# Which PSUM banks the last output-projection group takes in a hybrid decoder step

## The chip, the cores and the metric

The kernel runs on one core of one Trainium2 chip. The metric is device time in microseconds (us) of one execution. The engines are named as in the profile: PE is TensorE's matmul, PEld its weight load, DVE VectorE, ACT ScalarE, POOL GpSimd, SP SyncE, whose queue issues most loads. Time is told in us from the start of the span.

## What is computed

One layer of a decoder trunk for 512 prompt tokens and 8 single tokens of other sequences (520 columns in all, handled as two halves of 260): a SwiGLU feed-forward, a mixer with an output projection, a second SwiGLU, and a last norm. All is float32. Cut to what matters here:

```python
h = h + 0.5 * _swiglu(_rms_norm(h, ffn1_norm), ffn1_w_gate, ffn1_w_up, ffn1_w_down)
m, p, c, s = _hybrid_mixer(_rms_norm(h, mix_norm), ...)   # m = cat @ w_out, cat: pooled (512) and gated state-space (1024)
h = h + m                                                  # 1024 wide: 8 tiles of 128
h = h + 0.5 * _swiglu(_rms_norm(h, ffn2_norm), ffn2_w_gate, ffn2_w_up, ffn2_w_down)   # 2816 wide: 22 tiles f
```

## The kernel before

Features lie on the 128 partitions and tokens along the free axis, so `h` is 8 tiles (d = 0 to 7) of 128 x 520. A product in full precision is made of three matmuls of split operands: weights and inputs are each cut into a high part (a cast to the matmul's reduced format) and a low part (the rest), and high x high, high x low and low x high are added in a PSUM bank. The casts are made by ACT (`shi`, `whi`, `thi`), the low parts by DVE subtractions (`slo`, `wlo`, `tlo`) or, for some, by an accumulating DMA that POOL issues.

**The output projection** (`wout`) runs over three groups j of 512 input features and, in a group, over four weight loads d2, each for the two output tiles d = 2 d2 and 2 d2 + 1. For each d and each half b, twelve matmuls (eight at line 160, four at line 165) fill one bank, a tile named `wo{j}_{d}{b}`, and DVE adds it to `h` (line 1311). Below, `wo_50` is output tile 5, half 0, of the last group j = 2.

**The second feed-forward** (`Ffn` with i = 2) begins under that last group. Its first weight tile f = 0 is computed plainly in float32 (line 311, tiles `P_00` for the gate and `P_01` for the up projection; each float32 matmul shows as two rows in the trace), over four pairs j of input tiles (d = j and j + 4); `fin` squares and scales a finished `h` tile on ACT (`sq_f`, `xg_f`; the names of the pairs 0 to 3 end in 7345, 7379, 7505 and 7539), and `fill(j)` issues the pair's `P` matmuls and prepares its sums and differences (`xd_f`) with their high and low parts (`xth_f`, `xtl_f`) for the tiles f from 1 on. The order in which the stages are written is the string

```python
LAST_PLAN = "h0 h2 h1 n0 h3 n1 n2 n3"
```

where `h` is a call of `wout` with its d2 and `n` one of `fill`. So output tiles come in the order 0, 1, 4, 5, 2, 3, 6, 7.

The tiles f from 1 on save a multiplication by a seven-product scheme: a tile has an accumulator `A` (one bank) and a pair `BE` (two banks). Between products the partial sum in `A` is copied out by ACT (line 504), then the next product is added into the same bank. The last product of a tile f uses a quarter of its weights, `qs`, and is issued after the first product of tile f + 1. The first products of f = 1 use weights `whi_1a`, `shi_1c` and `shi_1d`; its third copy out of `A_1` goes to `ac_1_1`.

**Banks.** The pool that `open_f2` opens has eight banks: tag `ps` has two, tag `A` two, and tag `BE` two tiles of two banks. A tag's banks are taken in turn, and the next tile of a tag waits until the one two before it has been read. `P_00` and `P_01` take the two `BE` tiles. The tag `A` serves the accumulators of f = 1, 2 and so on.

**Order.** The program is written in the order of the plan, but the framework reorders instructions: a scheduler with a model of each engine decides the order on each engine's queue, apart from instructions that are pinned or made to be issued behind a given other. The queues themselves run in order. A change of buffers thus changes the order.

Of the kernel before, what the change touches and what calls it, by code (L numbers as in the profile page):

```python
# [897 lines left out]
def mixer(tc, ins, outs, e):  # L898
# [393 lines left out]
    def wout(cat, j, d2, fin=None):  # L1292
        src, name = ins["w_out"][j, d2], f"wo{j}{d2}"
        if (j, d2) in OUT_LOW_BY_DMA:
            raw = raw_tile(name)
            nc.sync.dma_start(out=raw, in_=src)
            wh, wl = e["weight_homes"](1024, name, wp, 3, ("whi", "wlo"))
            e["part_by_dma"](wh, wl, raw, src)
        else:
            wh, wl = load_unit(src, 1024, name, (*behind.get((j, d2), ()), *rows[-5:-4]) if (j, d2) == (2, 2)  # L1300
                               else behind.get((j, d2), ()))
        for d in (2 * d2, 2 * d2 + 1):
            for b, hs in enumerate(HALVES):
                if d != 1 or j != 2:
                    ps = bank(f"wo{j}_{d}{b}")
                else:
                    ps = e["ps"][0].tile([P, 512], F32, tag="A", bufs=2, name=f"wo{j}_{d}{b}")
                i = range((d % 2) * 4, (d % 2) * 4 + 4)
                mm_low_last(ps[:, :HB], *([ws(w, k) for k in i] for w in (wh, wl)),
                            *([cat[:, q, k, hs] for k in range(4)] for q in range(2)), True)  # L1310
                rows.append(nc.vector.tensor_tensor(out=h[:, d, hs], in0=ps[:, :HB], in1=h[:, d, hs], op=ALU.add).ins)  # L1311
                if fin is not None:
                    fin(d, b, hs)
# [49 lines left out]
    def outs_a():  # L1363
# [19 lines left out]
        "B": lambda j: ssd_b(*ssd(j)),  # L1383
        "z": zproj,
        "o": lambda j: wout(catp, 0, j),
        "G": gate,
        "H": gate_out,
        "g": lambda j: wout(cats[0], 1, j),
        "h": lambda j: wout(cats[1], 2, j, fin),
        "n": fill,  # L1390
        "e": lambda j: outs_a(),
# [101 lines left out]
```

## Time and profile before

| | us |
|---|---|
| median of 3 runs | 950.68 (949.75 to 951.92) |
| the profiled execution, its whole time | 952.73 |
| its span, from the first to the last instruction | 950.9 |
| mean granted TensorE clock | 0.997 |

The profile is of one execution. Busy time is the time in which an engine had an instruction under way; matmuls overlap, so the start of one row to the start of the next tells the cost of a matmul better than its length does. In the rows in order of time the columns are the start, the length, the engine, the line, the operation, the tile written and the tiles read, the shape and the number of instructions, and in brackets the idle time of the engine just before and what ended it.

### The profile page before, as it was taken

What the parts mean: (1) busy time and instruction counts of PE and PEld (TensorE: products, weight loads), DVE (VectorE), ACT (ScalarE), POOL (GpSimd) and SP (SyncE); (2) the same over time, 40 slices, a digit from 0 to 9 for tenths busy, and PEclk for the clock granted to TensorE, in tenths of its full rate; (3) what the DMA queues carried; (4) which work ended last, traced back from release to release, by engine and by line L of the source; (5) the groups of instructions that cost most, each with busy time, mean ns of one, the idle gap of its engine ahead of it and who ended that gap; (6) DMA issues with size and microseconds to landing.
All of it is one profiled execution on the core that took longest, in us unless ns stands there. A gap on an engine that the chain in (4) does not pass through costs nothing. (4 is left out here: it accounts for less than half of the span.)

```text
span 950.9 us, 19685 instructions
## 1 busy us (share of the span) xinstructions
PE 941.6 (99%) x7674; PEld 923.9 (97%) x7674; DVE 851.8 (90%) x1462; ACT 635.7 (67%) x1178; POOL 152.6 (16%) x230
## 2 busy tenths in 40 slices
PE   9999999999999999999999999999999999999996
PEld 8999999999999999999999899999999999999996
DVE  6899899998988698779998998999999999999986
ACT  7777756667566465475768745777776677766764
POOL 0011100100100002146251100111112101122120
PEclk9999999999999999999999999999999999999998
DMA  7666554455553335354364443546666655767642
GB/s 212 180 164 146 148 147 140 113 135 164 134 153 97 87 96 162 91 169 150 97 179 133 140 113 117 139 120 156 164 178 175 164 147 137 172 203 181 171 158 91
DMA packets 54123, 138.36 MB, mean 146 GB/s; under 512 B 7878, under 2 KB 16006, under 8 KB 54030
## 3 DMA queue, kind: packets, MB, share of 16 engines
q1 hardware_dynamic: 40046, 104.20, 34.6%
q0 software_dynamic: 13712, 32.78, 18.6%
q8 instruction: 60, 0.98, 0.4%
q14 instruction: 33, 0.27, 0.1%
q10 hardware_dynamic: 272, 0.13, 0.0%
HBM read 129.74 MB, written 7.34 MB: 144 GB/s over the span
## 5 line engine op out<-in xcount | busy, mean ns | idle before, releaser
L504 ACT COPY ac<-A 128x260 f32<-128x260 f32 x85 | 31.7, 373 | 34.6 <-PE A L165 16.4
L433 DVE TENSOR_TENSOR s<-raw 128x1024 f32<-128x1024 f32 x39 | 47.6, 1221 | 4.0 <-DMA raw<-in_w2gu 2.5
L504 ACT COPY ac<-BE 128x260 f32<-128x260 f32 x41 | 15.5, 377 | 33.4 <-PE BE L165 17.6
L151 PE MATMUL inx<-xh_mx,whi_inx 128*128 128x260 f32 x112 | 31.8, 284 | 0.0
L154 PE MATMUL inx<-xl_mx,whi_inx 128*128 128x260 f32 x112 | 31.6, 282 | 0.0
L155 PE MATMUL inx<-xh_mx,wlo_inx 128*128 128x260 f32 x112 | 31.6, 282 | 0.0
L1033 DVE SCALAR_TENSOR_TENSOR A<-U,h,A 128x544 f32<-128x544 f32 x36 | 28.4, 789 | 1.8 <-ACT A L1031 1.4
L311 PE MATMUL P<-x,raw 128*128 128x260 f32 x128 | 29.3, 390 | 0.0
L311 PEld LDWEIGHTS P<-x,raw 128*128 128x128 f32 x128 | 24.9, 196 | 3.9
L160 PE MATMUL wo<-catg,whi_wo 128*128 128x260 f32 x192 | 27.4, 285 | 0.0
L160 PEld LDWEIGHTS wo<-catg,whi_wo 128*128 128x128 f32 x192 | 24.8, 188 | 0.2
L139 ACT CAST thi<-raw 128x1024 fp32r<-128x1024 f32 (+1 forms) x14 | 14.2, 1014 | 15.5 <-PE wo L160 4.8
L1311 DVE TENSOR_TENSOR h<-wo,h 128x260 f32<-128x260 f32 x48 | 19.2, 423 | 4.9 <-PE wo L165 4.7
L1199 ACT ACTIVATE so<-br,sxdt 128x128 f32<-128x128 f32 x64 | 22.7, 375 | 1.2 <-DVE room L1201 0.7
L252 DVE TENSOR_TENSOR gs<-gq,gs 128x780 fp32r<-128x780 f32 (+1 forms) x28 | 23.2, 829 | 0.0
L151 PE MATMUL inz<-xh_mx,whi_inz 128*128 128x260 f32 x80 | 22.9, 287 | 0.0
L154 PE MATMUL inz<-xl_mx,whi_inz 128*128 128x260 f32 x80 | 22.7, 283 | 0.0
L155 PE MATMUL inz<-xh_mx,wlo_inz 128*128 128x260 f32 x80 | 22.6, 283 | 0.0
L512 DVE TENSOR_TENSOR BE<-BE,ac 128x260 f32<-128x260 f32 (+1 forms) x41 | 18.5, 451 | 3.1 <-PE BE L155 1.7
L151 PEld LDWEIGHTS inx<-xh_mx,whi_inx 128*128 128x128 f32 x112 | 21.1, 188 | 0.2 <-issue 0.2
L160 PE MATMUL A<-xth_f,qs 128*128 128x260 f32 x84 | 21.2, 283 | 0.0
L160 PE MATMUL A<-xtl_f,qs 128*128 128x260 f32 x84 | 21.2, 284 | 0.0
(3135 smaller groups left out, 4380.9 us busy)
## 6 DMA issues: line engine op xcount, KB each, us to landing
raw<-in_w2gu SPq DMA_DIRECT2D x44, 512.0 KB, 4.3
raw<-in_w1gu SPq DMA_DIRECT2D x41, 512.0 KB, 4.2
raw<-in_w_in SPq DMA_DIRECT2D x24, 512.0 KB, 3.6
raw<-in_w1d SPq DMA_DIRECT2D x16, 512.0 KB, 4.6
raw<-in_w2d SPq DMA_DIRECT2D x16, 512.0 KB, 4.3
raw<-in_w_out SPq DMA_DIRECT2D x12, 512.0 KB, 3.5
ab<-scr_acs SPq DMA_DIRECT2D x8, 512.0 KB, 6.3
h<-in_state_ssm SPq DMA_DIRECT2D x16, 256.0 KB, 3.7
```

What stands on the lines that cost most here:

```text
L151: first = nc.tensor.matmul(ps, whi, xhi, start=start, stop=False, **kw)
L154: nc.tensor.matmul(ps, whi, xlo, start=False, stop=False, **kw)
L155: nc.tensor.matmul(ps, wlo, xhi, start=False, stop=stop, **kw)
L160: mm = nc.tensor.matmul(ps, w, x, start=start, stop=False, **kw)
L252: low = nc.vector.tensor_tensor(out=lo, in0=s, in1=hi.bitcast(F32), op=ALU.subtract)
L311: mm = nc.tensor.matmul(self.banks[f, u][b][:, :HB], ws(self.raw[f][:, u], j + 4 * q), xg[:, slot[q]], start=j == q == 0, stop=j == 3 and ...
L433: nc.vector.tensor_tensor(out=s1, in0=diag, in1=up0, op=ALU.add)
L504: self.copied = nc.scalar.copy(keep, out[:, :HB]).ins
L512: nc.vector.tensor_tensor(out=be[:, s], in0=be[:, s], in1=a[:, s], op=ALU.add)
L1033: nc.vector.scalar_tensor_tensor(out=A[:, :n], in0=U[:, j : j + n], scalar=w(j), in1=A[:, :n], op0=ALU.mult, op1=ALU.add)
L1199: nc.scalar.activation(out=o[:, q], in_=br, func=AF.Copy, scale=sxdt[:, j, b : b + 1]))
L1311: rows.append(nc.vector.tensor_tensor(out=h[:, d, hs], in0=ps[:, :HB], in1=h[:, d, hs], op=ALU.add).ins)
```

## The change

In the last group, the two halves of every odd output tile (1, 3, 5, 7) take the two banks of tag `A`; the even ones keep the two banks of tag `ps`. Before, only output tile 1 took the banks of tag `A`, and the seven others shared those of tag `ps`.

```diff
         for d in (2 * d2, 2 * d2 + 1):
             for b, hs in enumerate(HALVES):
-                if d != 1 or j != 2:
+                if d % 2 == 0 or j != 2:
                     ps = bank(f"wo{j}_{d}{b}")
                 else:
                     ps = e["ps"][0].tile([P, 512], F32, tag="A", bufs=2, name=f"wo{j}_{d}{b}")
```

No instruction is added or removed. What the scheduler makes of it shows on PE first. Before, from the end of output tile 4 on, the fill of pairs 0 and 1 stands between the tiles (`thi`, `tlo` are weights, `catg` the projection's input, `xg_f` a pair's scaled input, a row with x2 is two matmuls):

```order
L165 MATMUL wo_41_7328<-catg_7093,tlo 128x260 x4
L311 MATMUL P_00_7451<-xg_f_7345,raw 128x260 x2
L311 MATMUL P_01_7456<-xg_f_7345,raw 128x260 x2
L160 MATMUL wo_50_7348<-catg_7093,thi 128x260 x8
L165 MATMUL wo_50_7348<-catg_7093,tlo 128x260 x4
L160 MATMUL wo_51_7362<-catg_7093,thi 128x260 x8
L165 MATMUL wo_51_7362<-catg_7093,tlo 128x260 x4
L311 MATMUL P_00_7451<-xg_f_7345,raw 128x260 x2
L311 MATMUL P_01_7456<-xg_f_7345,raw 128x260 x2
L311 MATMUL P_00_7451<-xg_f_7379,raw 128x260 x2
L311 MATMUL P_01_7456<-xg_f_7379,raw 128x260 x2
```

Now, at the end of the group on PE, the last tiles follow each other, and the fill of pairs 1, 2 and 3 comes behind them:

```order
L160 MATMUL wo_70_7508<-catg_7093,whi_wo_7470 128x260 x8
L165 MATMUL wo_70_7508<-catg_7093,wlo_wo_7471 128x260 x4
L160 MATMUL wo_71_7522<-catg_7093,whi_wo_7470 128x260 x8
L165 MATMUL wo_71_7522<-catg_7093,wlo_wo_7471 128x260 x4
L311 MATMUL P_00_7451<-xg_f_7379,raw 128x260 x4
L311 MATMUL P_01_7456<-xg_f_7379,raw 128x260 x4
L311 MATMUL P_00_7451<-xg_f_7505,raw 128x260 x2
```

Between these two places output tiles 5, 2 and 3 now run without a `P` matmul, and pair 0's eight `P` matmuls stand together behind tile 3. Of the 64 `P` rows of the trace, 40 stood ahead of the last tile, and 16 do now. Four matmuls of `A_1` that stood ahead of tile 7 now stand behind all of `P`.

On ACT the order moves too, also past the group's end. Before, at the first products of tile f = 1, the third copy out of `A_1` stands ahead of two casts of weights (`shi_2d` of tile 2 and `whi_3a` of tile 3; `gq_0` is the gate of f = 0):

```order
L504 COPY ac_1_0_7635<-A_1_7633 128x260
L139 CAST shi_2c<-s_2_2_7727 128x1024
L369 ACT_TABLE_LOAD
L369 ACTIVATE gq_0_7582<-gq_0_7582 128x2x260
L504 COPY ac_1_1_7636<-A_1_7633 128x260
L139 CAST shi_2d<-room 128x1024
L139 CAST whi_3a<-raw 128x1024
```

Now, at the same place on ACT:

```order
L504 COPY ac_1_0_7635<-A_1_7633 128x260
L139 CAST shi_2c<-s_2_2_7727 128x1024
L369 ACT_TABLE_LOAD
L369 ACTIVATE gq_0_7582<-gq_0_7582 128x2x260
L139 CAST shi_2d<-room 128x1024
L139 CAST whi_3a<-raw 128x1024
L504 COPY ac_1_1_7636<-A_1_7633 128x260
```

The copy now stands behind both casts. On DVE the evictions of line 1311 move ahead of the preparation of the pairs, and in the first tiles of the feed-forward some rows change places; on POOL one transfer (`wlo_1a`) moves ahead of another; the order on SP is the same.

## The prediction

> **What bounds the kernel now.** I read the page first, then the list of what TensorE waited for, then the table by stages around the change, then the rows in order of time.
>
> ```profile
> span 950.9 us, 19685 instructions
> PE 941.6 (99%) x7674; PEld 923.9 (97%) x7674; DVE 851.8 (90%) x1462; ACT 635.7 (67%) x1178; POOL 152.6 (16%) x230
> ```
> TensorE is busy for 99% of the span, so only two things can move the time: TensorE work, or a place where TensorE stands still. The list of its waits over the whole span (total, times, longest):
>
> ```profile
> PE warm L709 <- DVE eps L95: 1.1, 1, 1.1
> PE factor L870 <- PE psl L864: 0.6, 1, 0.6
> PE inz L151 <- DVE E L1278: 0.4, 1, 0.4
> PE psl L864 <- ACT sq_last L834: 0.3, 1, 0.3
> PE yo L1262 <- DVE hst L1275: 0.2, 1, 0.2
> PE px L1223 <- ACT X L1035: 0.2, 1, 0.2
> ```
> None is an output projection tile waiting for a bank. The stage, with the first five columns as busy time of PE, PEld, DVE, ACT and POOL (instructions), then the granted clock, DMA share and GB/s:
>
> ```profile
> 584.00:615.00 31.00, 31.00 (x205) 29.00 (x205) 27.17 (x46) 21.84 (x30) 4.99 (x6) 1.00 0.51 119
> 615.00:620.00 5.00, 5.00 (x43) 4.93 (x42) 4.97 (x5) 2.47 (x7) 0.00 (x0) 1.00 0.50 164
> 620.00:625.00 5.00, 5.00 (x44) 5.00 (x43) 5.00 (x8) 4.62 (x6) 0.00 (x0) 1.00 0.27 75
> ```
> TensorE is busy 31.00 of 31.00 us in the stretch in which the last group's tiles and the fill run. VectorE is nearly as full. Who waits for whom there is told by the group of the evictions (busy, mean ns | idle before, and what ended it):
>
> ```profile
> L1311 DVE TENSOR_TENSOR h<-wo,h 128x260 f32<-128x260 f32 x12 | 5.1, 424 | 2.2 <-PE wo L165 2.0
> ```
> VectorE waits 2.0 us for TensorE's tiles; TensorE waits for no eviction. With two banks the fill (`P`) stood between the tiles and covered the evictions.
>
> **The change part by part.** *Work on TensorE.* The same matmuls are issued, in other places: 40 of the 64 `P` rows and four of `A_1` stood ahead of the last tile, now only 16 do. Does it pay to break up a block less often?
>
> ```profile
> 584.66 1.92 PE L311 MATMUL P<-xg_f,raw 128*128 128x260 f32 x8
> 586.22 1.31 PE L160 MATMUL wo<-catg,thi 128*128 128x260 f32 x8
> 587.37 0.64 PE L165 MATMUL wo<-catg,tlo 128*128 128x260 f32 x4
> 587.84 1.13 PE L160 MATMUL wo<-catg,thi 128*128 128x260 f32 x8
> 589.28 3.67 PE L311 MATMUL P<-xg_f,raw 128*128 128x260 f32 x16
> 592.60 1.31 PE L160 MATMUL wo<-catg,whi_wo 128*128 128x260 f32 x8
> 594.23 1.12 PE L160 MATMUL wo<-catg,whi_wo 128*128 128x260 f32 x8
> ```
> From start to start, a tile alone takes 589.28 - 587.84 = 1.44. Eight `P` and a tile take 587.84 - 584.66 = 3.18, so the eight cost 1.74; sixteen and a tile take 594.23 - 589.28 = 4.95, so the sixteen cost 3.51. Twice 1.74 is 3.48: a switch costs nothing (-0.03). The longer first rows after `P` (1.31 for 1.12) are only an earlier start. Term: 0, bounds -0.1 and +0.1.
>
> *The banks.* `wo_50` now takes the bank of `wo_10`, and so on: each tile takes a bank whose eviction lies four tiles back, 5.7 us of TensorE time. An eviction is 0.42 (row above), and the longest queue that I find ahead of one on VectorE is some 2.5 us of other work; no wait. Term 0.
>
> *Fill and `A_1` behind the tiles.* Six tiles from 584.66 end at 593.3, 16 `P` at 596.8, four tiles at 602.6, then `P` for pairs 1 and 2 at 609.6. The last pair's scaled tiles need two evictions, a square and two scales behind `wo_71`, some 3 us of ACT and DVE work from 602.6, and are wanted at 609.6. The last `P` and the four rows of the sums of squares (0.22 each, as `P`) end at 614.0, `A_1`'s first product at 615.4; its bank is that of `wo_70`, long free. One new wait: VectorE's differences of pair 2 take the buffer of pair 1's scaled tile, whose `P` matmuls now run to 606.1 (before, they stood ahead of the last four tiles). Behind that wait VectorE has eleven operations, those of these two rows among them:
>
> ```profile
> 607.54 0.69 DVE L238 TENSOR_TENSOR xd_f<-xg_f 128x520 f32<-128x520 f32 x1
> 614.92 1.24 DVE L252 TENSOR_TENSOR xtl_f<-xd_f,xth_f 128x1040 fp32r<-128x1040 f32 x1
> ```
> Before, the stretch from the first to the end of the second was 8.6 us with one eviction and one addition more, about 1.0; so eleven from 606.2 end near 613.9, and with a wait for a cast that ACT can make only after its copy of `P_00`, at 615.2. The first matmul that needs it stands at 616.2. Before, it was late:
>
> ```profile
> 615.72 0.64 PE L165 MATMUL A<-xth_f,wlo_1a 128*128 128x260 f32 x4
> 616.21 0.39 PE L160 MATMUL BE<-xtl_f,shi_1c 128*128 128x260 f32 x1
> 616.44 0.64 PE L165 MATMUL BE<-xth_f,slo_1c 128*128 128x260 f32 x4
> ```
> 616.44 - 616.21 = 0.23 where two matmuls otherwise stand 0.12 apart: a gap of 0.11 as the operand ends at 616.16. It goes: -0.11, bounds -0.11 and +0.5 (VectorE 1.4 us later than I count).
>
> *What the order on ScalarE makes of it.* This is the largest term. `A_1`'s third copy (L504) must have read the bank before TensorE adds the last quarter (`qs`) into it. Before:
>
> ```profile
> 619.53 1.06 ACT L139 CAST shi_2c<-s 128x1024 fp32r<-128x1024 f32 x1 [0.58 <-PE BE L160]
> 620.60 1.28 ACT L369 ACT_TABLE_LOAD   x1
> 621.90 0.64 ACT L369 ACTIVATE gq<-gq 128x520 f32<-128x520 f32 x1
> 622.89 0.38 ACT L504 COPY ac<-A 128x260 f32<-128x260 f32 x1 [0.36 <-PE A L165]
> 623.16 1.05 ACT L139 CAST shi_2d<-room 128x1024 fp32r<-128x1024 f32 x1
> 624.12 1.06 ACT L139 CAST whi_3a<-raw 128x1024 fp32r<-128x1024 f32 x1
> 625.07 0.38 ACT L504 COPY ac<-A 128x260 f32<-128x260 f32 x1
> 622.09 0.28 PE L160 MATMUL A<-xtl_f,shi_1c 128*128 128x260 f32 x1
> 624.12 0.28 PE L160 MATMUL A<-xth_f,qs 128*128 128x260 f32 x1
> ```
> The copy was over at 623.27, 0.85 before the matmul at 624.12. Now both casts stand ahead of it. The chain to the activation is released by TensorE (619.53) and does not move against it. `shi_2d` can start when the activation is done (622.5) and the last matmul with `shi_1c` has ended (622.09 + 0.28); the casts step by 0.96 and 0.95 (623.16, 624.12, 625.07), so the copy starts at 624.4 and ends at 624.8: TensorE waits 0.65. Bounds: 0.5 if the casts close up, 0.9 if the release costs as much as the copy's own idle. Behind the waiting matmul stands all of TensorE. Nothing hides it.
>
> *Later.* One gap in the next tiles can take some of it back:
>
> ```profile
> 665.31 0.28 PE L160 MATMUL A<-xtl_f,qs 128*128 128x260 f32 x1
> 665.58 0.75 PE L165 MATMUL A<-xth_f,qs 128*128 128x260 f32 x4
> 657.31 0.86 POOL L248 DMA_DIRECT2D qs<-in_w2gu  x1 [0.32 <-ACT qs L247]
> ```
> There TensorE waits for a transfer asked for at 657.31: 0.27 for 0.12, 0.75 for 0.64 and 0.06 behind, together 0.3. If TensorE comes 0.5 later and the request moves less, the gap shrinks; but its casts wait for TensorE too, and a cast of `gs` now stands ahead. Between -0.3 and +0.3 I take -0.2. SP's order is unchanged; on POOL `wlo_1a`'s transfer moves ahead of one request (L430) whose result is first read near 620; I price that at 0, with at most 0.3 if it came late.
>
> Sum: 0 + 0 - 0.11 + 0.65 - 0.2 = +0.34. The profiled execution took 952.73 (950.9 of span, 1.8 around it); it is 2.05 above the median of 950.68, so the change is set against the median: 951.0.
>
> **The rivals.** *The copy is not late* (ScalarE reaches the casts sooner, or the bank is released otherwise): then -0.11 to -0.3 stays, 950.5. For it: ACT is idle 0.58 at 619.53. Against: that idle is ended by TensorE.
>
> *The banks were the bound.* If each of the twelve tiles had waited out an eviction, 12 x 0.42 = 5.1 us would go: 945.6. Against it stand 31.00 of 31.00 and the 2.0 us that VectorE waits for the tiles. The Trainium skill, Perfetto Trace Analysis (Matmul Optimizations), says to use all eight banks for the most parallelism; by that rule this change gains. The trace gives the rule no idle time to fill here, so its gain would be 0.
>
> *Slower: the third tile's weights.* `whi_3a` now stands ahead of the copy, and its raw buffer is loaded only when the last `P` has been read, at about 614.0 in both orders.
>
> ```profile
> raw<-in_w2gu SPq DMA_DIRECT2D x13, 512.0 KB, 4.0
> DMA to landing us min/median/max: 3.5/4.0/7.0
> ```
> It lands at 618.0 to 621.0, and is wanted at 623.4. From a landing of 9.4 us on, each further us holds ScalarE, the copy and TensorE for one us; 11 us would give +1.6 on top, 952.6. The longest seen is 7.0. The Trainium skill, TensorE: Matmul & The Clock Gate (A second HAM failure mode), reports that short idles between groups can make the clock swing; by that, the new gap would cost more than itself. The row of 615 to 620, with a gap of 0.11, has a clock of 1.00.
>
> **How the numbers follow.** Late copy, as worked out: 0.63 (951.0, own range 950.0 to 952.0). Copy not late: 0.22. Banks: 0.05. Late weights or another wait that I did not find: 0.10. A measurement here tells 0.2%, 1.9 us, from nothing: the first two cases lie within it but for the scatter of the runs (949.75 to 951.92), the third is faster, the fourth mostly slower: faster 0.05, same 0.87, slower 0.08. The range takes the first two with that scatter, 949.3 to 952.6.
>
> **What would show it.** Right: `wo` tiles 1.44 apart from 584.7 without `P` up to `wo_31`; no gap near 616; a new wait of TensorE near 624 on ACT's L504, 0.5 to 0.9 us; a clock of 1.00. Wrong: a TensorE wait on L1311 or on an xtl/xth row between 585 and 617, or no wait near 624.

## The result

The changed kernel is slower: 953.42 us, median of 13 runs (952.13 to 954.95), against 951.45 for the kernel before in the same session (13 runs, 949.75 to 953.63). The ratio is 1.0019, 95% interval 1.0012 to 1.0027, or +1.8 us (1.1 to 2.6). A second series of the same kernel gave 1.0024 (1.0014 to 1.0034). The forecast was +0.3 us and "same". Its base, the median of three runs, was 0.8 below the median of thirteen, so even the right difference would have been read from a low base. The profiled execution of the changed kernel took 953.39.

The page after, span and busy time by engine:

```profile
span 951.6 us, 19689 instructions
PE 942.1 (99%) x7674; PEld 924.1 (97%) x7674; DVE 850.5 (89%) x1462; ACT 635.2 (67%) x1178; POOL 152.3 (16%) x230
```

The counts of each engine's work are those of before; the four instructions more are waits for semaphores. The table by stages, columns as before: the last group and the fill are as full as they were (31.00 of 31.00), and the clock is 1.00. What is new lies behind them, 4.54 of 5.00 in the stretch from 620 on:

```profile
584.00:615.00 31.00, 31.00 (x205) 29.01 (x204) 27.81 (x47) 22.20 (x32) 4.99 (x6) 1.00 0.52 128
615.00:620.00 5.00, 5.00 (x44) 5.00 (x43) 4.93 (x5) 2.19 (x5) 0.00 (x0) 1.00 0.30 106
620.00:625.00 5.00, 4.54 (x38) 4.33 (x38) 4.30 (x6) 4.48 (x7) 0.00 (x0) 1.00 0.33 105
```

In the list of TensorE's waits two lines are new, both for a copy of partial sums on ScalarE (total, times, longest):

```profile
PE A L160 <- ACT ac L504: 0.5, 1, 0.5
PE BE_Down(c=0, d=0)_8646 L160 <- ACT BE_Down(c=0, d=0)_8646 L504: 0.4, 1, 0.4
```

The first is the wait that was forecast. The rows of ScalarE, then those of TensorE:

```profile
621.43 0.64 ACT L369 ACTIVATE gq<-gq 128x520 f32<-128x520 f32 x1
621.97 1.04 ACT L139 CAST shi_2d<-room 128x1024 fp32r<-128x1024 f32 x1
622.91 1.04 ACT L139 CAST whi_3a<-raw 128x1024 fp32r<-128x1024 f32 x1
623.86 0.65 ACT L504 COPY ac<-A 128x260 f32<-128x260 f32 x2
623.18 0.63 PE L165 MATMUL A<-xth_f,wlo_2a 128*128 128x260 f32 x4
624.28 0.39 PE L160 MATMUL A<-xth_f,qs 128*128 128x260 f32 x1 [0.46 <-ACT ac L504]
624.51 0.28 PE L160 MATMUL A<-xtl_f,qs 128*128 128x260 f32 x1
```

Four matmuls from 623.18 would end their turn at 623.66 (0.12 each); the next starts at 624.28, and the one behind it 0.23 later instead of 0.12: 0.62 + 0.11 = 0.73 lost.

The second I did not forecast. It lies at the down projection of the first chunk, whose first copy must fill half of `BE_Down(c=0, d=0)`, to which TensorE adds its next product. ScalarE before:

```profile
694.60 0.63 ACT L251 CAST gs<-gq 128x520 fp32r<-128x520 f32 x1
695.24 0.36 ACT L504 COPY BE_Down(c=0, d=0)_8646<-A_Down(c=0, d=0)_8645 128x260 f32<-128x260 f32 x1
695.51 1.06 ACT L397 ACTIVATE wlo_Down(c=0, d=1)a<-whi_Down(c=0, d=1)a 128x1024 fp32r<-128x1024 f32 x1
```

ScalarE after, and TensorE's row that waits:

```profile
695.06 0.64 ACT L251 CAST gs<-gq 128x520 fp32r<-128x520 f32 x1
695.59 1.07 ACT L397 ACTIVATE wlo_Down(c=0, d=1)a<-whi_Down(c=0, d=1)a 128x1024 fp32r<-128x1024 f32 x1
696.55 0.38 ACT L504 COPY BE_Down(c=0, d=0)_8646<-A_Down(c=0, d=0)_8645 128x260 f32<-128x260 f32 x1
696.98 1.22 PE L160 MATMUL BE_Down(c=0, d=0)_8646<-gs,shi_Down(c=0, d=0)c 128*128 128x260 f32 x8 [0.35 <-ACT BE_Down(c=0, d=0)_8646 L504]
```

The negated weights of the next tile (L397, 1.07 us) now stand ahead of the copy; TensorE loses 0.62 from start to start. Both executions together: +0.73 and +0.62, less the gaps near 616 (0.11), 665 (0.27) and 817 (0.11) that are gone, and four single gaps of some 0.09 that came, make about +1.2 us. From the first matmul of output tile 4 in the group j = 1, some 12 us ahead of the last `wo` group, to the sums of squares of the end it is

```profile
564.40 1.31 PE L160 MATMUL wo<-catg,thi 128*128 128x260 f32 x8
933.09 0.60 PE L873 MATMUL psl<-acc_last,ones 128*128 128x260 f32 x2
```

before, 368.69 us, and after

```profile
564.10 1.31 PE L160 MATMUL wo<-catg,thi 128*128 128x260 f32 x8
933.83 0.60 PE L873 MATMUL psl<-acc_last,ones 128*128 128x260 f32 x2
```

369.73. This length (below: the late stage) leaves out what the earlier stages do from one execution to the next. Its +1.04 is less than the +1.8 of the runs; where the rest can be, the experiments show in part.

### The profile page after: what moved, and what is told of

Read it like the earlier page. It is cut to its first block, busy times and chain, and to the rows that moved or that the text cites. A ratio compares the mean times of both kernels' runs of the same rounds, so it can differ in the third digit from the quotient of the medians.

```text
span 951.6 us, 19689 instructions
## 1 busy us (share of the span) xinstructions
PE 942.1 (99%) x7674; PEld 924.1 (97%) x7674; DVE 850.5 (89%) x1462; ACT 635.2 (67%) x1178; POOL 152.3 (16%) x230
## 5 line engine op out<-in xcount | busy, mean ns | idle before, releaser
L504 ACT COPY ac<-A 128x260 f32<-128x260 f32 x85 | 31.6, 373 | 33.9 <-PE A L155 16.7
L504 ACT COPY ac<-BE 128x260 f32<-128x260 f32 x41 | 15.5, 377 | 34.5 <-PE BE L165 18.9
L1199 ACT ACTIVATE so<-br,sxdt 128x128 f32<-128x128 f32 x64 | 22.5, 375 | 4.0 <-DVE room L1201 2.9
L1311 DVE TENSOR_TENSOR h<-wo,h 128x260 f32<-128x260 f32 x48 | 19.2, 424 | 2.7 <-PE wo L165 2.7
L251 ACT CAST gs<-gq 128x780 fp32r<-128x780 f32 (+1 forms) x28 | 20.6, 737 | 1.4 <-DVE gq L555 0.9
```

The lines of the kernel that those rows point to most:

```text
L251: cast = nc.scalar.copy(hi, s)
L504: self.copied = nc.scalar.copy(keep, out[:, :HB]).ins
L1199: nc.scalar.activation(out=o[:, q], in_=br, func=AF.Copy, scale=sxdt[:, j, b : b + 1]))
```

## The experiments

Theory after the first profile: the two late copies on ScalarE cost the time, and the banks do not. Rivals: the banks and the places of the `P` blocks cost it; or the rest of the changed order does, since between the two traces the order on ScalarE differs in some 90 rows and that on VectorE in over 200, a moved row counted where it stood and where it stands.

**Two of the three tiles that the change moves.** Tile 1 had the banks of tag `A` before, so the change moves tiles 3, 5 and 7. Here tile 7 keeps its old banks:

```diff
-                if d % 2 == 0 or j != 2:
+                if d not in (1, 3, 5) or j != 2:
```

> Output tiles 1, 3 and 5 take the other banks and tile 7 keeps its own: three quarters of the change, and by the order both late copies (the third one of A_1, and that of Down(0,0)) stand ahead of the casts again, as they did before. Theory of the two late copies: both new TensorE waits (0.73 us near 624, 0.62 near 697) are absent, and the time is that of the kernel before, -0.4 to +0.3 us. Rival, the banks and the places of the P blocks themselves cost the time: +1.0 to +1.8 us against before. Rival, the rest of the changed order behind tile 3 costs it: also about that of before, since that order is close to the old one here.

> Output tiles 1, 3 and 5 on the other banks once more, the version that came out fastest (0.9992 of before, interval 0.9983 to 1.0000). If its gain is from the gaps that are gone (0.27 near 665, 0.11 near 616), it is -0.3 to -0.6 us again, ratio 0.9993 to 0.9997, and the second profile shows at most 0.15 us of TensorE gaps in the second feed-forward. If the first result was chance: ratio 0.9997 to 1.0005.

Measured: 0.9992 (0.9983 to 1.0000), and again 1.0002 (0.9994 to 1.0011): no difference from before. The first profile lists no TensorE wait in the late stage (368.21 us). The second has two (370.09 us), so my 0.15 us for it was wrong: the gain of the first series is not to be had reliably. One is a copy of L504 that comes late although the orders on ScalarE and VectorE are here those of the kernel before, from the copy of `Down(0,0)` on; TensorE loses 1.2 us. VectorE, then ScalarE:

```profile
876.11 1.23 DVE L433 TENSOR_TENSOR s<-raw 128x1024 f32<-128x1024 f32 x1 [2.90 <-DMA raw<-in_w2gu]
879.26 0.37 ACT L539 ACTIVATE BE<-BE 128x260 f32<-128x260 f32 x1 [2.10 <-DVE BE L529]
880.11 0.38 ACT L504 COPY ac<-A 128x260 f32<-128x260 f32 x1
```

A weight transfer landed late, and what ScalarE had ahead of the copy waited for VectorE. Two of the three moved tiles, with `P` placed nearly as in the changed kernel, do not cost the 1 to 1.8 us of the rival.

**The copy of `Down(0,0)` ahead of L397, the change whole.** The edit binds one instruction:

```diff
-                    nc.scalar.activation(out=lo[:, n2:], in_=hi[:, n2:].bitcast(F32), func=AF.Copy, scale=-1.0)
+                    with queued(*((self.copies[(0, 0), 1],) if (i, f) == (2, (0, 1)) else ())): nc.scalar.activation(out=lo[:, n2:], in_=hi[:, n2:].bitcast(F32), func=AF.Copy, scale=-1.0)
```

It moved much more than that pair. From the copy of `Down(0,0)` to the end, the rows of L504, L1199, L396 and L397 on ScalarE come out in exactly the order of the kernel before; TensorE's order stays that of the changed kernel. VectorE's order moves back as well: behind that place it differs from before in some 100 rows in the changed kernel, and in 14 with the binding. Ahead of it nothing moves on either engine. So the runs with this binding test the two orders together.

> The whole change, with Down(0,1)'s negated weights (L397) made to be issued after the copy of Down(0,0); the third copy of A_1 stays behind the two casts. The rest of the order falls close to that of before. Theory of the two late copies: the wait near 697 goes and the one near 624 stays, +0.4 to +0.8 us against before. Rival, the banks and the P blocks: +1.5 to +1.9 as the changed kernel. Rival, the rest of the changed order: -0.3 to +0.3 and the wait near 624 is taken back later.

> The whole change with the copy of Down(0,0) ahead of L397 once more (1.0004 of before the first time, interval 0.9995 to 1.0013), for a second profile and a tighter time. It keeps the late third copy of A_1 with its wait of 0.73 near 624. Theory: ratio 1.0003 to 1.0010, that is +0.3 to +0.9 us for the late copy less the gaps that are gone; the stage from the last wo group to the end shows few waits besides that of 0.73. Rival, ScalarE's order is not what costs the changed kernel its time: ratio 1.0015 to 1.0025.

Measured: 1.0004 (0.9995 to 1.0013) and 1.0005 (0.9995 to 1.0015), +0.4 us, with the late stage at 369.20 and 369.70. In both, the only TensorE wait listed in the late stage is that of the late third copy:

```profile
PE A L160 <- ACT ac L504: 0.5, 1, 0.5
```

Against the changed kernel's 1.0019 and 1.0024 that is 0.0017 less, some 1.6 us (give or take 0.9, the intervals combined). TensorE's order and the banks are the changed kernel's, so they are not the cause by themselves: what stands behind the copy of `Down(0,0)` on ScalarE and VectorE holds nearly the whole loss. The late third copy costs 0.73 us in each of the four profiles that have it; the gaps near 616 and 665 that go pay back about half.

**Tiles 1, 5 and 7: early third copy, late copy of `Down(0,0)`.**

> Output tiles 1, 5 and 7 take the other banks and tile 3 keeps its own. By the order the third copy of A_1 is early, as before, and the copy of Down(0,0) stands behind Down(0,1)'s negated weights, as in the changed kernel; most of the rest of the order is that of the changed kernel. Theory of the two late copies: no wait near 624, the wait near 697 stays, +0.3 to +0.7 us against before. Rival, the rest of the changed order: +1.0 to +1.9. Rival, the banks and the P blocks: +1.0 to +1.8.

Measured: 1.0026 (1.0015 to 1.0037), +2.5 us: far more than the +0.3 to +0.7 of my theory, and above the rivals' ranges too, though its interval (+1.4 to +3.5) reaches into them. The late copy of `Down(0,0)` by itself is not the account. TensorE's waits in the late stage (372.98 us):

```profile
PE BE_Down(c=1, d=2)_10461 L160 <- ACT c_Down(c=1, d=2)_1_10463 L504: 0.9, 1, 0.9
PE BE_Down(c=0, d=0)_8646 L160 <- ACT BE_Down(c=0, d=0)_8646 L504: 0.8, 1, 0.8
PE BE L160 <- ACT BE L504: 0.7, 2, 0.4
PE P L311 <- ACT xg_f L234: 0.6, 1, 0.6
PE A_Down(c=0, d=2)_8914 L160 <- ACT ac_Down(c=0, d=2)_0_8916 L504: 0.2, 1, 0.2
```

Four of the five lines are copies of L504. They lie behind the copy of `Down(0,0)` or are it, apart from one of the two of `BE`, near 656, where weights came late to ScalarE; the order there is the same in the next run, which does not show that wait. Here too the rows of L504, L1199, L396 and L397 behind it stand exactly as in the changed kernel. With the one constraint of the run above added, TensorE's order unchanged:

> Output tiles 1, 5 and 7 on the other banks, as in the run that took 1.0026 of before, and Down(0,1)'s negated weights (L397) made to be issued after the copy of Down(0,0). TensorE's order stays word for word that run's; ScalarE's order of copies, weight casts and state products from there on becomes word for word that of the kernel before. Theory, the loss is in that order: the wait near 697 is gone and the waits behind it mostly too, 1.5 to 2.4 us less than without the edit, ratio 1.0000 to 1.0010 (the gap of 0.8 us near 607, which belongs to its P blocks, stays). Rival, the loss is in TensorE's order or the banks: ratio 1.0020 to 1.0030 as without the edit.

Measured: 1.0007 (0.9997 to 1.0017), 0.0019 or 1.8 us less than without it (give or take 1.4); the late stage is 370.20, and the copies' waits are gone from the list. What stays is the `P` wait near 607 (1.1 us this time). The theory is now: the loss belongs to the order on ScalarE from the copy of `Down(0,0)` on. That VectorE's order, which goes back with it, has a part in it is a rival that no run here tells apart.

**The casts behind the third copy, the change whole.** `shi_2d` and `whi_3a` are issued after it:

```diff
-                    d1 = split(raw[:, 0], 1024, f"{n}a", wp, 3, ("whi", "wlo"))
+                    with queued(*((self.copies[1, 7],) if (i, f) == (2, 3) else ())): d1 = split(raw[:, 0], 1024, f"{n}a", wp, 3, ("whi", "wlo"))
...
-            e2 = split(s2, 1024, f"{n}d", wx, 2, ("shi", "slo"))
+            with queued(*((self.copies[1, 7],) if (i, f) == (2, 2) else ())): e2 = split(s2, 1024, f"{n}d", wx, 2, ("shi", "slo"))
```

> The whole change, with the casts of shi_2d and whi_3a made to be issued after the third copy of A_1; by the order the copy of Down(0,0) comes early with it, and the rest of the order is neither that of before nor that of the changed kernel. Theory of the two late copies: both waits are gone, and with the gaps near 616, 665 and 817 gone too the time is -0.5 to +0.2 us against before. Rival, the banks and the P blocks: +0.5 to +1.8. Rival, the rest of the changed order: +0.5 to +1.5.

Measured: 1.0007 (0.9998 to 1.0017), late stage 370.65. Both early copies did not bring the promised -0.5 to +0.2: its profile has other waits, among them 0.4 us for the transfer of `wlo_Down(c=1, d=0)`, 0.3 for VectorE's `gs` and 0.3 for a copy of L504 in tile 19. By its interval this run cannot tell the promise from the rivals. But TensorE's order is the changed kernel's throughout, and ScalarE's and VectorE's are from tile f = 13 on; against the changed kernel it is 0.0014 less (give or take 0.0011). So the new order from tile 13 on does not hold the whole loss: at least a part of it lies ahead of that, at the two late copies and in the tiles between.

**Tile 7 alone.** Tiles 3 and 5 keep the `ps` banks, and tile 1, which had those of tag `A` before, goes back to `ps`:

> Only output tile 7 takes the other banks; tiles 1, 3 and 5 keep their own, so a quarter of the change with tile 1 undone as well. By the order the third copy of A_1 is early, and the copy of Down(0,0) stands behind Down(0,1)'s negated weights, as in the changed kernel and in the run with tiles 1, 5 and 7; most of the rest of ScalarE's order is theirs too. Theory, the cost follows ScalarE's order behind the copy of Down(0,0): a wait near 697 of 0.5 to 1.1 us, other new waits for ScalarE's copies behind it, +1.0 to +2.6 us against before. Rival, it follows how many tiles change banks: at most a third of the changed kernel's loss, 0 to +0.6 us.

Measured: 1.0079 (1.0066 to 1.0092), +7.5 us, though only tile 7 moves to new banks: the cost does not follow the number of tiles, but I had priced it far too low, and tile 1's return to `ps` is in it. Its waits in the late stage:

```profile
PE P L311 <- ACT xg_f L234: 2.9, 1, 2.9
PE wo L160 <- DVE h L1311: 0.8, 1, 0.8
PE BE_Down(c=0, d=0)_8646 L160 <- ACT BE_Down(c=0, d=0)_8646 L504: 0.7, 1, 0.7
```

Tile 7 moves up, its first half ahead of tile 5 and its second ahead of tile 2; `P` of the later pairs is reached before its scaled tile is made; and tile 1, back on `ps`, waits for an eviction. So the places of the `P` blocks can cost time, in this kernel though not in the changed one, where neither line appears. With the constraint on L397:

> Only output tile 7 on the other banks, as in the run that took 1.0079 of before, with the same edit to L397. TensorE's order stays that run's. Theory: 1.5 to 2.4 us less than without the edit, ratio 1.0050 to 1.0065; what is left are its own waits near 576 (1.1 us, for VectorE's L1311) and near 607 to 613 (some 4.8 us, for ScalarE's xg_f), which belong to where that kernel puts tile 7 and the P blocks. Rival, the rest of that kernel's loss comes from that order too: ratio below 1.004. Rival, the order does nothing: 1.0070 to 1.0090.

Measured: 1.0054 (1.0037 to 1.0071). The fall of 0.0025 has the sign and size of the others, but the two intervals overlap; this pair alone would not settle it. Its late stage is longer than without the binding (376.90 against 375.49), and two copies of L504 are late in the old order too, at `Down(1,2)` (TensorE loses 0.5 us) and `Down(1,3)` (0.9).

**Where the rest of the time is: the same two kernels profiled again.**

> The changed kernel once more, for a second profile and a second time. Open from its first profile: the trace of the second feed-forward shows 1.2 us more TensorE gaps than before, the runs took about 1.8 us more. If the gaps are set by the order of ScalarE's instructions, the waits near 624 (0.73) and 697 (0.62) return within 0.1 us, and what differs between the two profiles lies elsewhere. If they are set by the transfers, they change by some tenths. Time: +1.2 to +2.4 us against before.

> The kernel before once more, for a second profile. If its few gaps in the second feed-forward (0.11 near 616, 0.27 near 665, 0.11 near 817) are set by the order, they return; if the one near 665, which waits for a transfer of qs, is set by the transfers, it differs by 0.1 us or more. The gaps near 506 and 531 in the mixer (0.66 and 0.51 in the first profile) differ between executions in either case. Ratio 1.000.

The kernel before came out at 1.0006 (0.9997 to 1.0015), late stage 369.24. Its gaps near 616 (0.10) and 665 (0.25) returned; gaps of 0.23, 0.36 and 0.17 near 719, 738 and 816 were new or longer. The changed kernel took 954.78 in this execution, late stage 372.95, 3.2 us longer than in its first. Its wait near 622 is the same 0.73; that of `Down(0,0)` is 0.88, which is not within the 0.1 that I expected; and there are others:

```profile
PE BE_Down(c=1, d=2)_10461 L160 <- ACT c_Down(c=1, d=2)_1_10463 L504: 0.8, 1, 0.8
PE BE_Down(c=0, d=0)_8646 L160 <- ACT BE_Down(c=0, d=0)_8646 L504: 0.6, 1, 0.6
PE A L160 <- ACT ac L504: 0.5, 1, 0.5
PE BE L160 <- ACT BE L504: 0.4, 1, 0.4
PE A_Down(c=1, d=2)_10460 L165 <- DMA wlo_Down(c=1, d=2)a<-in_w2d: 0.4, 1, 0.4
PE A_Down(c=0, d=2)_8914 L160 <- ACT ac_Down(c=0, d=2)_0_8916 L504: 0.2, 1, 0.2
```

Four of them are L504 waits of the run with tiles 1, 5 and 7, which has the same order there. Of the 3.2 us, some 2.0 lie at copies that the change put behind other work: 1.1 at `Down(1,2)`, 0.6 at `BE` of tile 9, 0.3 more at `Down(0,0)`. The rest lies mostly where the order is that of before (0.5 at the copy of `Down(0,2)`) or where TensorE waits for a transfer itself (0.65, `wlo_Down(c=1, d=2)`). The longest, followed back in this execution, VectorE first, then ScalarE, then TensorE:

```profile
838.29 1.23 DVE L433 TENSOR_TENSOR s_Down(c=1, d=3)_10582<-raw 128x1024 f32<-128x1024 f32 x1 [2.65 <-DMA raw<-in_w2d]
841.31 0.34 DVE L1201 SCALAR_TENSOR_TENSOR room<-room,sdec,so 128x128 f32<-128x128 f32 x1
841.68 0.37 ACT L1199 ACTIVATE so<-br,sxdt 128x128 f32<-128x128 f32 x1 [2.77 <-DVE room L1201]
841.99 0.37 ACT L504 COPY c_Down(c=1, d=2)_1_10463<-BE_Down(c=1, d=2)_10461 128x260 f32<-128x260 f32 x1
842.41 1.23 PE L160 MATMUL BE_Down(c=1, d=2)_10461<-gs,shi_Down(c=1, d=2)d 128*128 128x260 f32 x8 [0.82 <-ACT c_Down(c=1, d=2)_1_10463 L504]
```

A weight transfer lands late; VectorE waits 2.65 us for it, and its state update (L1201) stands behind. ScalarE's state product (L1199) needs the buffer which that update reads, and waits 2.77. The copy for TensorE stands behind the product. In the kernel before, the two stand the other way round:

```profile
839.15 0.38 ACT L504 COPY c_Down(c=1, d=2)_1_10463<-BE_Down(c=1, d=2)_10461 128x260 f32<-128x260 f32 x1 [1.34 <-PE BE_Down(c=1, d=2)_10461 L165]
839.42 0.38 ACT L1199 ACTIVATE so<-br,sxdt 128x128 f32<-128x128 f32 x1
```

There the copy is released by TensorE itself, and a late transfer holds the product behind it, and with that the next copy, which stands behind the product in both orders. The kernel with tile 7 alone and L397 bound shows it: its copy ran at 844.51, its product waited 1.92 until 846.81, and the next copy cost the 0.5 us named above. The Trainium skill, TensorE: Matmul & The Clock Gate (Architectural detail), says that ScalarE's and VectorE's queues are strictly first in, first out; these rows agree, since the copy starts 0.31 behind the start of L1199, though the product that it copies was done by 840.16:

```profile
839.52 0.64 PE L165 MATMUL BE_Down(c=1, d=2)_10461<-gs,slo_Down(c=1, d=2)c 128*128 128x260 f32 x4
```

So the order in the changed kernel costs a part that is there each time, the late copy of `Down(0,0)` (0.62 to 1.04 in the four profiles that have it), and a part that depends on when transfers land in that execution (near nothing in the first profile, some 2 us in the second). Late transfers cost the old order something too, as tiles 1, 3 and 5 showed. The second part can be where the 0.8 us were which the first profile lacked; two profiles do not show it. How the average splits between the two was not measured by itself: the constraint removes both at once.

## The late stage, kernel by kernel

| kernel | order on ScalarE and VectorE from the copy of `Down(0,0)` on | ratio of the runs | late stage, us |
|---|---|---|---|
| before | old | 1, 1.0006 | 368.69, 369.24 |
| tiles 1, 3, 5 | old | 0.9992, 1.0002 | 368.21, 370.09 |
| the change, L397 bound | old but for a few rows | 1.0004, 1.0005 | 369.20, 369.70 |
| tiles 1, 5, 7, L397 bound | old but for a few rows | 1.0007 | 370.20 |
| the change, casts bound | a third one, new from tile 13 on | 1.0007 | 370.65 |
| **the change** | new | 1.0019, 1.0024 | 369.73, 372.95 |
| tiles 1, 5, 7 | new | 1.0026 | 372.98 |
| tile 7, L397 bound | old but for a few rows | 1.0054 | 376.90 |
| tile 7 | new | 1.0079 | 375.49 |

Each late stage is of one execution and scatters by up to 3 us within one kernel; the ratios decide. None of the kernels is measurably faster than the one before.

## Why the prediction was wrong

- *Work on TensorE, 0.* Right: tiles without `P` between them start 1.44, 1.42 and 1.45 apart, and the stretch is full.

```profile
587.22 1.12 PE L160 MATMUL wo<-catg,whi_wo 128*128 128x260 f32 x8
588.66 1.11 PE L160 MATMUL wo<-catg,whi_wo 128*128 128x260 f32 x8
590.08 1.12 PE L160 MATMUL wo<-catg,whi_wo 128*128 128x260 f32 x8
591.53 1.11 PE L160 MATMUL wo<-catg,whi_wo 128*128 128x260 f32 x8
```

- *The banks, 0.* Right: no wait for L1311 in the changed kernel. Four banks in place of two brought no gain, as that rival's line said they could not. Where tile 1 went back to `ps` (tile 7 alone), a tile did wait for its bank.
- *Fill and `A_1`, -0.11.* Right: the row with `slo_1c` follows its neighbour after 0.12, and no operand is late between 585 and 617.
- *ScalarE's order, +0.65.* Right for the one place that I worked out: 0.73.
- *Later, -0.2.* The gap near 665 did go (-0.27), but this is the step that failed: it counts one gap and nothing else behind 625. The difference of the two orders on ScalarE showed L397 ahead of the copy of `Down(0,0)`, with TensorE's next product behind that copy, the same pattern that I had just priced at 0.65; that place alone cost 0.62 in the first profile and 0.88 in the second. I did not carry the search past the first place. The order behind that copy, on ScalarE and VectorE together, is worth 1.6 us (0.9 either way) in the runs. With it bound back the kernel is at +0.4, where the sum had +0.34; with intervals of 0.9 either way, that they agree to 0.1 is luck.
- *The rivals.* "Another wait that I did not find" got a share of 0.10 together with late weights, and the range ended at 952.6. Some 90 rows of difference on the queue that makes the copies for TensorE, and over 200 on VectorE's, deserved more. `whi_3a`'s weights were not late, and the clock did not swing (1.00 across both new waits).
- *The base.* 950.68, a median of three, was 0.8 below that of thirteen; the range, set around it, was low by as much. Set around 951.45 it would have ended at 953.4, where the changed kernel's median lies, so the base put that median outside; the forecast of the change itself, +0.34 for +1.8, fell short without it.

## What to carry over

When an edit changes how a scheduler orders an in-order engine that TensorE depends on, list every place in the whole program where a long instruction or one with a wait of its own has moved ahead of a copy that frees or fills a bank, and price each; one found early is no reason to stop. An instruction whose wait hangs on a transfer can cost more ahead of such a copy than a long one (1.1 us against 0.88 in one execution here), and one profile may show none of it. If the new order is the trouble, one binding where it leaves the old can bring the old order back, and tells the order from the edit. See on every engine what else the binding moved: here it was VectorE's order too.

## What the runs showed of the hardware

The pause of 2.9 us near 607 in the kernel with tile 7 alone lowered the granted clock behind it. Its table by stages (the clock is third from the end) and the row of the matmuls that follow the pause:

```profile
606.00:610.00 4.00, 1.21 (x11) 1.00 (x9) 3.07 (x5) 3.43 (x6) 0.00 (x0) 1.00 0.60 117
610.00:614.50 4.50, 4.39 (x12) 3.54 (x13) 4.50 (x9) 2.21 (x4) 0.86 (x1) 0.62 0.37 58
614.50:618.00 3.50, 3.50 (x18) 3.03 (x17) 2.41 (x3) 1.70 (x3) 0.00 (x0) 1.00 0.41 118
610.11 5.25 PE L311 MATMUL P<-xg_f,raw 128*128 128x260 f32 x15 [2.90 <-ACT xg_f L234]
```

Fifteen `P` took 5.25 us there; in the kernel before, sixteen took 3.67. With L397 bound as well, the pause was 2.97 us and the clock 0.50 in the 4.5 us and 0.66 in the 3.5 us behind that. If the low clock is 0.50 each time, these means make some 3.4 us of it in the first kernel and some 6.9 in the second, by estimate, after nearly the same pause. Pauses of up to 1.2 us (near 607 with tiles 1, 5 and 7 and L397 bound) left it at 1.00. The Trainium skill, TensorE: Matmul & The Clock Gate (Why this matters for your kernels), asks for no idle gap of TensorE beyond about 3 us, since one window of idle halves the clock; the trace agrees, with 2.9 us already enough here. The swing by short idles that the prediction cited from the same page of the Trainium skill did not show in any of these kernels: in all but the two with tile 7 alone the clock averaged 0.996 to 0.998.
